# Sixteen experts on one core: row indices found two experts ahead, rows gathered one ahead, and a second norm in steps

## The chip, the cores and the metric

The kernel runs on one core of a Trainium2 chip. The metric is the device time of one execution in microseconds; the kernel before takes 2919.67 us (median of 3 runs, 2919.27 to 2936.29). The engines are TensorE (PE, matmuls, with PEld for its weight loads), VectorE (DVE), ScalarE (ACT), GpSimd (POOL) and SyncE (SP, which issues plain DMAs). Each works through its own list of instructions in order and waits for the others by semaphores.

## The reference

One layer of an encoder for 2048 tokens of 1024 channels, all float32. Four mixers (retention, RWKV-7, RG-LRU, gated linear attention) run side by side on the channels of a normed input; an output projection and a residual follow. Then comes the part that the change touches, in which each of 16 experts takes the 256 tokens with the largest affinity for it:

```python
def _expert_choice_ffn(x, router_w, router_b, w_gate, w_up, w_down):
    ...
    gates, idx = lax.top_k(jnp.swapaxes(aff, 1, 2), cap)
    bidx = jnp.arange(B)[:, None, None]
    xs = x[bidx, idx]
    hid = jax.nn.silu(jnp.einsum('becd,edf->becf', xs, w_gate)) * jnp.einsum('becd,edf->becf', xs, w_up)
    out = jnp.einsum('becf,efd->becd', hid, w_down) * gates[..., None].astype(x.dtype)
    return jnp.zeros_like(x).at[bidx, idx].add(out.astype(x.dtype))
```

Its result is added to the residual, and a final norm over the channels of each token gives the output.

## The kernel before

The mixers, the output projection and the choice of tokens (`top_k`) take the time up to about 1700 us. They are the same in both kernels. The rest is `experts` (L1441).

*Precision.* A float32 product is made as three products of float32r parts. `split` (L41) copies a tile to its high part on ACT (L43) and subtracts it on DVE for the low part (L44). `mm3` (L122) then issues three matmuls of 128 x 256 for each of eight row tiles (L129).

*Weights.* Each expert reads twelve tiles of 1 MB: four quarters each of gate, up and down. `weights` (L1448) loads one into x_st by SP and splits it into x_wh (ACT) and x_wl (DVE), each with three buffers.

*The choice of rows.* `select(e)` (L1458) does four things in one piece. DVE writes sixteen tiles x_oh that mark which token stands at which place of expert e (L1462, one buffer). PE multiplies them with the token numbers, 32 small products (L1466). DVE turns the sums into x_idx (L1468, L1469). Then POOL gathers the 256 rows of the normed tokens from g.hf into x_xs by two indirect DMAs (L1471, in `gather`, L1576). PE turns x_xs in 16 transposes (L1478), four to a bank of PSUM (two such banks), and ACT and DVE split each bank into x_xh and x_xl.

*The loop over experts (L1485).* For each expert: 384 gate and up products in eight groups of 48. After each group ACT makes the silu (x_sg), DVE multiplies, and the result is split into x_hh and x_hl. Then `select(e + 1)` is called (L1505), and then come 192 down products in four quarters, whose results ACT scales by the gate into x_os (L1527). The row scales stand in x_xs, so x_xs (two buffers) is in use until the expert's last x_os. Two scatter-adds (L1543, L1585) by POOL add x_os to g.acc in DRAM, the second after the first has landed.

*The final norm.* `final_norm` (L1564) norms 256 tokens at a time beside experts 11 to 13. Tokens that get more from experts 11 to 14 are normed again by `renorm` (L1588): gather from g.acc into fn_x (two buffers), squares on ACT (fn_sq, L1560), rstd and scaling on DVE, scatter to the output. L1509 does it for experts 11 to 13 in expert 14, and for 14 in expert 15:

```python
        while late and e >= NE - 2:
            renorm(g, late.pop())
```

The rows of expert 15 itself are normed as its down products finish (L1529 to L1541).

*What sets the order.* The program is not put on the engines as it is written. A scheduler goes through it with a simulated timeline and decides which instruction of each engine's list stands next. So a call that is written between gate and down products can end up among the down products, and the listing below shows the result.

Of the kernel before, what the change touches and what calls it, by code (L numbers as in the profile page):

```python
# [17 lines left out]
P = 128  # L18
# [6 lines left out]
IN_XA = 3328                # columns of w_in of the GLA decay's input  # L25
# [15 lines left out]
def split(g, hi, lo, src, pool=False):  # L41
    """hi + lo == src exactly, both exact in float32r."""
    g.nc.scalar.activation(out=hi, in_=src, func=AF.Copy)  # L43
    (g.nc.gpsimd if pool else g.nc.vector).tensor_tensor(out=lo, in0=src, in1=hi.bitcast(F32), op=OP.subtract)  # L44
# [6 lines left out]
def rstd_of(g, pool, ss, n, scale, eps, name):  # L51
    """1 / sqrt(ss * scale + eps) for [P, n] sums of squares: a guess from the bits of the
    number (within 4%), and three Newton steps, which leave 1e-10 of that."""
# [14 lines left out]
def head_norm(g, pool, y, n, center, eps):  # L68
    """Normalises y [P, n, 64] over the last axis, in place."""
# [14 lines left out]
def load_h_block(g, b):  # L84
    """Normalised, transposed, split activations of 512 tokens."""
# [36 lines left out]
def mm3(g, out, lhs, rhs, lsl, rsl, nk=KD):  # L122
    """out = lhs.T @ rhs over nk row tiles in three float32r passes; outs and lsls may be
    lists, the outs then parts of one bank (the first start clears it for all)."""
# [7 lines left out]
def proj_cm(g, w, n, h, store):  # L132
    """channel-major projections of a 512-token block"""
    for m0 in range(0, n, P):
        m = min(P, n - m0)
        ps = bank(g)
        mm3(g, ps[:m, :], w, h, slice(m0, m0 + m), slice(0, 512))
        o = g.op.tile([P, 512], F32, name="o_cm", tag="o_cm")
        g.evac(o[:m, :], ps[:m, :])
        store(m0 // P, o[:m, :])  # L140
        yield
# [12 lines left out]
def stage_proj(g, d):  # L154
# [6 lines left out]
    # channel-major: lru input and gate, gla q and k, the gates of retention and gla  # L161
# [37 lines left out]
    def pair(js, blocks, then=(None, None), loaded=False):  # L199
        """Two sets of columns; a block of activations is replaced while the other one is used."""  # L200
# [40 lines left out]
# ----------------------------------------------------------------- RWKV-7  # L241
C = 64
NB = T // P
RS = 256                  # tokens of one elementwise step
HALF = 10 * C             # of one block's row of the RWKV scratch: r1 k1 b1 b0 k0 r0, z, v with its chunks swapped, of two heads
# [4 lines left out]
def rwkv_consts(c):  # L250
# [4 lines left out]
    # strict masks are negative: the triangular systems are kept as I - N  # L255
    c["m_at"] = np.stack([-(p < j).astype(f), -(p > j).astype(f)], 1)            # [P, dir, 64]
# [48 lines left out]
def rwkv_a(g, dr, t0, ao):  # L305
    """Elementwise work of RS tokens in direction dr, the products of the triangular
    systems, all of it left in DRAM scratch block by block."""
# [20 lines left out]
    other = None                   # the other direction's bonus, when it has been here before  # L328
# [6 lines left out]
    def chunks(q, u):  # L335
        """chunks u and 5 - u of half q"""
# [29 lines left out]
    # sigmoid(u) = (1 + tanh(u / 2)) / 2: aa is kept as twice the sigmoid less one, k and en carry the factors 2 and 1/2  # L366
    nc.gpsimd.tensor_scalar(out=sw, in0=sw, scalar1=0.5, scalar2=0.5, op0=OP.mult, op1=OP.add)
    # decay inside each chunk
# [13 lines left out]
    # norm of kk  # L382
# [42 lines left out]
    # decay of every chunk, the channels of each head on both halves of the partitions  # L425
    nc.vector.tensor_copy(out=g.pcx[:, dr, t0 // P:t0 // P + nb, :, :, :].rearrange("p b q h n -> p h q b n"),
                          in_=ps[:, 0:4 * nch].rearrange("p (h q b n) -> p h q b n", h=2, q=2, n=2))
    # bonus
# [12 lines left out]
    # the triangular systems  # L441
# [27 lines left out]
def rwkv_inv(g, n, eng):  # L469
    """Inverts the triangular systems of 4 blocks of each direction.  On the partitions: direction, half of the  # L470
    system (that with no other to wait for first), chunk, block, head; as in ao the chunks are swapped."""
# [20 lines left out]
def rwkv_join(g, n, ao, pool, bl):  # L492
    """The remaining quarter of each inverse, from its diagonal blocks x0, x1 and the quarter ao of the
    system: x0 ao x1."""
# [4 lines left out]
    def blocks(c, dr, r, k):  # L499
        """rows r, columns k of the inverses of chunk 1 - c"""  # L500
# [36 lines left out]
def rwkv_b_buffers(g):  # L537
    """Buffers whose fixed parts are written once."""
# [46 lines left out]
def rwkv_prep(g, dr, b, loaded, res):  # L585
    """Everything of one 128-token block that does not wait for the state: the matrix
    that takes [state; values] to [outputs; next state] for each chunk and head.  Chunk 0
    keeps the state on partitions 0..63, chunk 1 on 64..127."""
# [4 lines left out]
    bk = [[ld[:, HALF * q + 192 - 128 * e:HALF * q + 320 - 128 * e] for e in range(2)] for q in range(2)]     # b and k of a chunk, b where the chunk is  # L593
# [27 lines left out]
    rd = turn(g.rd)                # r of two heads, block-diagonal: half, 1 - chunk, head  # L621
# [71 lines left out]
def weave(*gens):  # L693
    """Generators with the number of steps of each, in proportion."""
# [20 lines left out]
def rwkv_b(g):  # L715
# [4 lines left out]
    for i in range(1, NB + 2):  # L720
# [26 lines left out]
        # tokens that both directions have passed: norm now, the rest a round later  # L747
# [11 lines left out]
def rwkv_out(g, m):  # L759
    """Norm, bonus and gate of 256 tokens."""  # L760
# [28 lines left out]
# ----------------------------------------------------------------- retention  # L789
def ret_consts(c):  # L790
    i = np.arange(128)
    f = np.float32
    rel = (i[None, :] - i[:, None]).astype(f)          # [j, i]: i - j
# [16 lines left out]
PI_1 = 6.28125                          # 2 pi in three parts, the first two exact in products  # L810
# [6 lines left out]
def ret_tables(g):  # L817
# [3 lines left out]
    lgs = pool.tile([P, 2, 2], F32, name="rt_lgs")        # [direction, q]: heads 2 q and 2 q + 1 on the halves of the partitions  # L821
# [3 lines left out]
    # positions -> sine and cosine  # L825
# [6 lines left out]
    g.cs = pool.tile([P, NB, 2, 32], F32, name="rt_cs")    # cos, cos  # L832
    g.sn = pool.tile([P, NB, 2, 32], F32, name="rt_sn")    # -sin, sin
# [15 lines left out]
    # decays  # L849
# [21 lines left out]
def rotate(g, pool, b, src, n):  # L871
    """Rotary embedding of n heads of 64 in src."""
# [11 lines left out]
def retention(g):  # L884
    """Blocks of 128 tokens; a first sweep from the right for the backward states, a second
    one from the left for the rest.  Two heads share the partitions: their states and
    queries are block-diagonal."""
# [15 lines left out]
    def state(e, b, rk, v):  # L903
        """S becomes the state after block b"""
# [69 lines left out]
def gated_out(g, pool, y4, j, gate, gn, k0):  # L974
    """mixed rows k0, k0 + 1 of 512 tokens: y * gn * silu(gate), channel-major"""
# [12 lines left out]
# ----------------------------------------------------------------- RG-LRU  # L988
def lru(g, q):
# [18 lines left out]
    # s8 = -8 softplus(-lambda): max(-l, 0) + log1p(exp(-|l|)), the logarithm by its series in y / (2 + y)  # L1008
# [20 lines left out]
    # convolution over t - 2 .. t + 1  # L1029
# [9 lines left out]
    for dr in range(2):  # L1039
# [13 lines left out]
        # 1 - a^2 = tanh(-log a) (1 + a^2)  # L1053
# [16 lines left out]
# ----------------------------------------------------------------- GLA  # L1070
# [7 lines left out]
GB = 2                      # blocks of 128 tokens in one elementwise step  # L1078
# [3 lines left out]
def gla(g):  # L1082
# [13 lines left out]
    cc = big.tile([P, 2, 3, NB], F32, name="gl_cc")     # decays up to a block's middle, of a block, from its middle on  # L1096
    SX = big.tile([P, NB, HD], F32, name="gl_SX")
    S = [big.tile([P, HD], F32, name=f"gl_S{e}") for e in range(2)]      # [(head, k), v]
# [3 lines left out]
    def piece(j):  # L1102
        """decayed q and k of GP tokens in both directions, centred on the middle of each block"""
# [45 lines left out]
    def products(o, e, v):  # L1149
        """keys times values of the piece's blocks, which the states take up"""  # L1150
# [12 lines left out]
    def state(e, b, kv):  # L1163
        """S becomes the state after block b"""
# [3 lines left out]
    def diag(e, b, src):  # L1168
        """the state decayed to the middle of block b, block-diagonal"""
# [271 lines left out]
def experts(g):  # L1441
# [43 lines left out]
    for e in range(NE):  # L1485
# [23 lines left out]
        while late and e >= NE - 2:  # L1509
            renorm(g, late.pop())  # L1510
# [261 lines left out]
```

## Time and profile before

| | |
|---|---|
| time, median of 3 runs | 2919.67 us (2919.27 to 2936.29) |
| span of the profiled execution, first to last instruction | 2917.0 us |
| PE busy | 2575.3 us, 88% of the span |
| DVE, ACT, POOL busy | 1803.9, 1380.3, 731.2 us |
| DMA | 525.83 MB, 180 GB/s |

The page gives the profiled execution's span, and no other time of its own; the median of the timed runs is 2.7 us above that span. A matmul's end in the trace is modelled and matmuls overlap, so the busy time of PE is not read as speed; the starts of the matmuls and their number in a stretch are. The granted clock of PE has two levels, 1.00 (2.4 GHz) and 0.50 (1.2 GHz).

### The profile page before, as it was taken

The page shows a single profiled execution, that of the slowest core. Times are in us where ns is not written, and L with a number is a line of the kernel's source. Part 1 is how long each engine was busy: PE and PEld are TensorE (multiplying, and loading weights), DVE is VectorE, ACT ScalarE, POOL GpSimd, SP SyncE. Part 2 cuts the span into 40 slices and gives each one's busy share as a digit, 9 for nine tenths or more (in the row PEclk, how much of TensorE's full clock was granted, in tenths as well). Part 3 has the DMA queues.
Part 4 walks back from the last instruction along what each step waited for, and adds up shares of the span by engine and source line. Part 5 has one row for each costly group of instructions (what it writes and reads, how often), then busy time and mean ns, then how long its engine had stood idle before and what let it go on. Part 6 is the DMA issues. An engine that isn't in the chain of part 4 may idle for free. (4 is left out here: it accounts for less than half of the span.)

```text
span 2917.0 us, 47393 instructions
## 1 busy us (share of the span) xinstructions
PE 2575.3 (88%) x18433; PEld 2306.9 (79%) x18433; DVE 1803.9 (62%) x3462; ACT 1380.3 (47%) x2303; POOL 731.2 (25%) x764
## 2 busy tenths in 40 slices
PE   7999998888878898895899659999999999999987
PEld 5886686667667787774677459999999999999987
DVE  4244467878888778788654565555555555566655
ACT  4126666545534676555433224444444444454453
POOL 0001112544544554436534300000000000000121
PEclk9999999999988899897999879999999999999999
DMA  9342255576455554435254426666666666688874
GB/s 319 116 157 90 101 184 174 194 218 196 123 138 158 166 164 149 141 122 187 88 185 148 160 88 199 201 197 205 206 208 203 198 193 193 212 295 273 267 244 151
DMA packets 473569, 525.83 MB, mean 180 GB/s; under 512 B 129504, under 2 KB 415232, under 8 KB 472576
## 3 DMA queue, kind: packets, MB, share of 16 engines
q1 hardware_dynamic: 461536, 479.54, 50.7%
q0 software_dynamic: 11808, 43.26, 5.8%
q8 instruction: 145, 2.38, 0.3%
q14 instruction: 80, 0.66, 0.1%
HBM read 387.97 MB, written 136.84 MB: 180 GB/s over the span
## 5 line engine op out<-in xcount | busy, mean ns | idle before, releaser
L44 DVE TENSOR_TENSOR x_wl<-x_st,x_wh 128x2048 fp32r<-128x2048 f32 x189 | 432.9, 2291 | 342.6 <-ACT x_wh L43 342.2
L129 PE MATMUL bank<-x_xl,x_wh 128*128 128x256 f32 x2048 | 567.3, 279 | 0.0
L129 PE MATMUL bank<-x_xh,x_wh 128*128 128x256 f32 x2048 | 565.6, 279 | 1.9 <-ACT x_wh L43 1.8
L129 PE MATMUL bank<-x_xh,x_wl 128*128 128x256 f32 x2048 | 562.5, 279 | 2.0 <-DVE x_wl L44 1.8
L43 ACT ACTIVATE x_wh<-x_st 128x2048 fp32r<-128x2048 f32 x192 | 368.0, 1918 | 88.5 <-PE bank L129 69.1
L129 PEld LDWEIGHTS bank<-x_xh,x_wh 128*128 128x128 f32 x2048 | 387.2, 190 | 2.6 <-ACT x_wh L43 2.2
L129 PEld LDWEIGHTS bank<-x_xl,x_wh 128*128 128x128 f32 x2048 | 385.0, 188 | 0.0
L129 PEld LDWEIGHTS bank<-x_xh,x_wl 128*128 128x128 f32 x2048 | 381.4, 188 | 3.0 <-DVE x_wl L44 2.8
L129 PE MATMUL bank<-x_wh,x_hh 128*128 128x256 f32 x1024 | 290.4, 286 | 9.6 <-ACT x_hh L43 9.2
L129 PE MATMUL bank<-x_wl,x_hh 128*128 128x256 f32 x1024 | 293.8, 288 | 0.0
L129 PE MATMUL bank<-x_wh,x_hl 128*128 128x256 f32 x1024 | 291.3, 286 | 0.0
L129 PE MATMUL bank<-h_hi,w_hi 128*128 128x512 f32 x576 | 237.8, 415 | 24.7 <-DVE o_tm L1622 9.1
L129 PE MATMUL bank<-h_lo,w_hi 128*128 128x512 f32 x576 | 236.4, 410 | 0.0
L129 PE MATMUL bank<-h_hi,w_lo 128*128 128x512 f32 x576 | 233.9, 406 | 0.0
L1576 POOL DMA_INDIRECT x_xs<-hf,x_idx x32 | 51.5, 1608 | 617.6 <-issue 530.7
L129 PEld LDWEIGHTS bank<-x_wh,x_hh 128*128 128x128 f32 x1024 | 196.1, 192 | 10.0 <-ACT x_hh L43 9.4
L129 PEld LDWEIGHTS bank<-x_wl,x_hh 128*128 128x128 f32 x1024 | 197.8, 193 | 0.0
L129 PEld LDWEIGHTS bank<-x_wh,x_hl 128*128 128x128 f32 x1024 | 197.6, 193 | 0.0
L129 PE MATMUL bank<-w_hi,h_hi 128*128 128x256 f32 (+1 forms) x512 | 157.4, 307 | 28.2 <-DVE o_tm L1622 13.5
L129 PEld LDWEIGHTS bank<-h_hi,w_hi 128*128 128x128 f32 x576 | 111.4, 194 | 60.4 <-DVE o_tm L1622 10.6
L129 PE MATMUL bank<-w_hi,h_lo 128*128 128x256 f32 (+1 forms) x512 | 154.0, 301 | 0.0
L129 PE MATMUL bank<-w_lo,h_hi 128*128 128x256 f32 (+1 forms) x512 | 152.2, 297 | 0.0
(449 smaller groups left out, 5573.4 us busy)
## 6 DMA issues: line engine op xcount, KB each, us to landing
x_st<-in_exp_w_gate_dram SPq DMA_DIRECT2D x64, 1024.0 KB, 5.3
x_st<-in_exp_w_up_dram SPq DMA_DIRECT2D x64, 1024.0 KB, 5.5
x_st<-in_exp_w_down_dram SPq DMA_DIRECT2D x64, 1024.0 KB, 5.4
w_st<-in_w_in_dram SPq DMA_DIRECT2D x24, 1024.0 KB, 5.8
rw_sp<-sp SPq DMA_DIRECT2D x16, 1280.0 KB, 5.7
bld<-rw_sp SPq DMA_DIRECT2D x32, 640.0 KB, 5.1
ld<-rw_cm SPq DMA_DIRECT2D x14, 899.5 KB, 6.4
cm<-o_cm SPq DMA_DIRECT2D x40, 256.0 KB, 3.5
```

The costliest lines, as they stand in the source:

```text
L43: g.nc.scalar.activation(out=hi, in_=src, func=AF.Copy)
L44: (g.nc.gpsimd if pool else g.nc.vector).tensor_tensor(out=lo, in0=src, in1=hi.bitcast(F32), op=OP.subtract)
L129: g.nc.tensor.matmul(out, lhsT=lhs[a][:, k, lsl], rhs=rhs[b][:, k, rsl], start=(k + i == 0 and out is outs[0]), stop=(3 * k + i == 3 * nk ...
L1576: g.nc.gpsimd.indirect_dma_start(out=t[:, s], out_offset=None, in_=src, in_offset=bass.IndirectOffsetOnAxis(ap=idx[:, s:s + 1], axis=0))
```

## The change

`select` is cut into `places` (x_oh, products, x_idx), `fetch` (the gather) and `turned`, which turns a quarter of the rows at each step. The indices of expert e + 2 are found in expert e, between its gate and its down products. The rows of expert e + 1 are gathered when expert e begins, and turned in quarters after the second, third and fourth quarter of expert e's gate and up products and once more behind them. x_idx has six buffers where it had four.

`renorm` becomes `renorm_all`, a generator that gathers one expert's rows ahead of the norm of the one before. It makes one step after each quarter of the gate and up products and after each quarter of the down products of experts 14 and 15. Experts 11 to 13 are normed in that order, where it was 13 to 11. Comments and docstrings are dropped, which moves line numbers.

```diff
-    def select(e):
-        idx = g.exs.tile([P, 2], I32, name="x_idx", bufs=4)
+    def places(e):
+        idx = g.exs.tile([P, 2], I32, name="x_idx", bufs=6)
...
         nc.vector.tensor_tensor(out=idx, in0=pv, in1=ps[:, 1:4:2], op=OP.add)
+        return idx
+
+    def fetch(idx):
         xs = g.exs.tile([P, 2, HROW], F32, name="x_xs")
         gather(g, xs, g.hf, idx)
+        return xs
+
+    def turned(xs):
...
             split(g, hi[:, k:k + 2], lo[:, k:k + 2], ps.rearrange("p (m t) -> p m t", m=2))
-        return idx, xs, hi, lo
+            yield hi, lo
...
-    nxt = select(0)
+    idx = places(0)
+    xs = fetch(idx)
+    for xh, xl in turned(xs):
+        pass
+    ahead_idx = places(1)
     late, done, fss = [], [], {}
+    again = iter(())
     for e in range(NE):
-        idx, xs, xh, xl = nxt
+        if e + 1 < NE:
+            xs1 = fetch(ahead_idx)
+            turn1 = turned(xs1)
...
+            if e + 1 < NE and m:
+                xh1, xl1 = next(turn1)
...
+            if e >= NE - 2:
+                next(again, None)
         if e + 1 < NE:
-            nxt = select(e + 1)
+            xh1, xl1 = next(turn1)
+            nidx = places(e + 2) if e + 2 < NE else None
...
-        while late and e >= NE - 2:
-            renorm(g, late.pop())
...
+            if e >= NE - 2:
+                next(again, None)
         if e < NE - 1:
             scatter(g, g.acc, os, idx, compute_op=OP.add)
             if e >= NE - LATE:
                 late.append(idx)
+            if e == NE - 3 or e == NE - 2:
+                again = renorm_all(g, late)
+                late = []
+        if e + 1 < NE:
+            idx, xs, xh, xl = ahead_idx, xs1, xh1, xl1
+            ahead_idx = nidx
...
-def renorm(g, idx):
-    t = g.fn.tile([P, 2, D], F32, name="fn_x")
-    gather(g, t, g.acc, idx)
+def renorm_all(g, idxs):
+    ts = []
+    for idx in idxs:
+        t = g.fn.tile([P, 2, D], F32, name="fn_x")
+        gather(g, t, g.acc, idx)
+        ts.append((t, idx))
+        yield
+        if len(ts) == 2:
+            again(g, *ts.pop(0))
+            yield
+    while ts:
+        again(g, *ts.pop(0))
+        yield
+
+def again(g, t, idx):
     norm_rows(g, t, squares(g, t, 2))
     scatter(g, g.out, t, idx)
```

The scheduler makes the following of it. On PE, the first transposes of expert 1's rows (x_xs) stand in the kernel before among expert 0's down products (x_wh and x_wl with x_hh and x_hl), behind 79 of them and the 32 products with x_oh:

```order
L129 MATMUL bank<-x_wh,x_hl 128x256
L129 MATMUL bank<-x_wh,x_hh 128x256 x2
L1478 MATMUL bank<-c_ident,x_xs 128x128 x2
L129 MATMUL bank<-x_wl,x_hh 128x256
L129 MATMUL bank<-x_wh,x_hl 128x256
```

In the changed kernel they stand among the gate and up products (x_xh and x_xl with x_wh and x_wl):

```order
L129 MATMUL bank<-x_xl,x_wh 128x256
L129 MATMUL bank<-x_xh,x_wl 128x256
L1486 MATMUL bank<-c_ident,x_xs 128x128 x4
L129 MATMUL bank<-x_xh,x_wh 128x256
L129 MATMUL bank<-x_xl,x_wh 128x256
```

What moved: four transposes stand behind 192 gate and up products of the expert, four behind 288, and eight behind all 384. Then come 59 down products, the 32 products with x_oh for the expert after the next, and the other 133 down products. Before, the 32 products stood between gate and down products, and the transposes at four places among the down products.

On POOL, at the start of the expert stage, with the numbers of the tiles (x_idx_15202 and x_idx_15771 are those of experts 0 and 1, acc_82 is g.acc), before:

```order
L1576 DMA x_xs_15256<-hf_83,x_idx_15202 128x1040 x2
L1576 DMA x_xs_15825<-hf_83,x_idx_15771 128x1040 x2
L1585 DMA acc_82<-x_os_15858,x_idx_15202 2048x1024 x2
L1576 DMA x_xs_16625<-hf_83,x_idx_16571 128x1040 x2
L1585 DMA acc_82<-x_os_16658,x_idx_15771 2048x1024 x2
```

And in the changed kernel, where x_idx_15289 is expert 1's and x_idx_15858 expert 2's:

```order
L1603 DMA x_xs_15256<-hf_83,x_idx_15202 128x1040 x2
L1603 DMA x_xs_15343<-hf_83,x_idx_15289 128x1040 x2
L1612 DMA acc_82<-x_os_15912,x_idx_15202 2048x1024
L1603 DMA x_xs_16143<-hf_83,x_idx_15858 128x1040 x2
L1612 DMA acc_82<-x_os_15912,x_idx_15202 2048x1024
L1612 DMA acc_82<-x_os_16712,x_idx_15289 2048x1024
```

What moved: the gather of expert 2's rows stands between the two scatter-adds of expert 0, where it stood behind both, and needs indices that were found an expert earlier.

On ACT, in expert 15, whose second norm of expert 14's rows is fn_sq of fn_x (the squares of its two halves), before:

```order
L1498 ACTIVATE x_sg_27687<-bank_27638 128x256
L43 ACTIVATE x_hh_27570<-x_sg_27687 128x256
L1498 ACTIVATE x_sg_27753<-bank_27704 128x256
L43 ACTIVATE x_hh_27570<-x_sg_27753 128x256
L43 ACTIVATE x_wh_27820<-x_st_27818 128x2048
L1560 ACTIVATE fn_sq_28059,fn_ss_28058<-fn_x_28055 128x1024
L43 ACTIVATE x_wh_27934<-x_st_27932 128x2048
```

And in the changed kernel:

```order
L1513 ACTIVATE x_sg_27687<-bank_27638 128x256
L1587 ACTIVATE fn_sq_27816,fn_ss_27815<-fn_x_27692 128x1024
L43 ACTIVATE x_hh_27570<-x_sg_27687 128x256
L1513 ACTIVATE x_sg_27756<-bank_27707 128x256
L43 ACTIVATE x_hh_27570<-x_sg_27756 128x256
L43 ACTIVATE x_wh_27847<-x_st_27845 128x2048
L1587 ACTIVATE fn_sq_27818,fn_ss_27815<-fn_x_27692 128x1024
```

What moved: the first fn_sq stands directly behind the second x_sg of the expert, ahead of two x_hh and of the x_wh of the third up quarter; before, it stood behind them. On POOL the gather into that fn_x stands ahead of the gather into x_fx, where it stood behind it, and the third gather into fn_x in expert 14 stands behind two scatters to the output, where it stood behind three.

## Rows read from the trace of the kernel before

**Rows 1.** The page, busy tenths of PE in 40 slices of the span.

```profile
PE   7999998888878898895899659999999999999987
```

**Rows 2.** Waits of PE, 1750 to 2917 us: total us, times, longest us.

```profile
PE bank L1478 <- DMA x_xs<-hf,x_idx: 36.8, 13, 3.4
PE bank L129 <- ACT x_hh L43: 9.2, 1, 9.2
PE bank L129 <- DVE x_wl L44: 1.8, 3, 0.8
PE bank L129 <- ACT x_wh L43: 1.8, 2, 1.4
```

**Rows 3.** Timeline of PE, 2065.8 to 2071: start, us, line; in brackets idle before.

```profile
2066.55 0.39 PE L129 MATMUL bank<-x_wh,x_hh 128*128 128x256 f32 x2
2069.91 0.42 PE L1478 MATMUL bank<-c_ident,x_xs 128*128 128x128 f32 x2 [2.97 <-DMA x_xs<-hf,x_idx]
```

**Rows 4.** Timeline of POOL: gathers of two experts, scatter-adds between them.

```profile
2061.64 2.20 POOL L1576 DMA_INDIRECT x_xs<-hf,x_idx  x1 [38.88 <-issue]
...
2085.86 1.61 POOL L1585 DMA_INDIRECT acc<-x_os,x_idx  x1 [20.76 <-ACT x_os L1527]
2092.91 1.59 POOL L1585 DMA_INDIRECT acc<-x_os,x_idx  x1 [5.43 <-DVE x_hl L44]
2133.32 2.50 POOL L1576 DMA_INDIRECT x_xs<-hf,x_idx  x1 [38.83 <-issue]
```

**Rows 5.** Timeline of DVE, 2054 to 2072.

```profile
2058.05 2.44 DVE L1462 TENSOR_SCALAR x_oh<-x_iota,tk_slot 128x256 bf16<-128x256 bf16 x12
...
2060.66 2.29 DVE L44 TENSOR_TENSOR x_wl<-x_st,x_wh 128x2048 fp32r<-128x2048 f32 x1
```

**Rows 6.** Windows: length, busy us (instructions) of PE, PEld, DVE, ACT, POOL, PEclk, DMA, GB/s.

```profile
1924.68:1928.10 3.42, 3.42 (x19) 3.42 (x18) 1.17 (x1) 3.42 (x6) 0.00 (x0) 0.50 0.02 5
1928.10:1931.51 3.41, 3.41 (x31) 3.41 (x31) 3.40 (x4) 2.31 (x3) 0.00 (x0) 1.00 0.29 92
...
2658.55:2665.38 6.83, 5.64 (x27) 5.67 (x28) 1.42 (x1) 4.09 (x6) 0.00 (x0) 0.50 0.58 237
2808.74:2818.98 10.24, 4.64 (x21) 4.64 (x22) 4.58 (x15) 4.92 (x8) 3.67 (x4) 0.50 0.67 249
```

**Rows 7.** Windows, L129 on PE alone: busy us (matmuls), PEclk, DMA, GB/s.

```profile
1730.00:1750.00 20.00, 20.00 (x179) 1.00 0.64 210
...
2236.00:2256.00 20.00, 20.00 (x172) 1.00 0.73 207
```

**Rows 8.** Timeline of ACT in experts 14 and 15.

```profile
2811.12 1.06 ACT L1560 ACTIVATE fn_sq<-fn_x 128x1024 bf16<-128x1024 f32 x1 [12.01 <-DMA fn_x<-acc,x_idx]
...
2813.89 0.40 ACT L43 ACTIVATE x_hh<-x_sg 128x256 fp32r<-128x256 f32 x1
...
2851.51 0.39 ACT L1498 ACTIVATE x_sg<-bank 128x256 f32<-128x256 f32 x1 [1.82 <-PE bank L129]
...
2853.10 1.92 ACT L43 ACTIVATE x_wh<-x_st 128x2048 fp32r<-128x2048 f32 x1 [0.30 <-PE bank L129]
2858.28 1.06 ACT L1560 ACTIVATE fn_sq<-fn_x 128x1024 bf16<-128x1024 f32 x1 [3.26 <-DMA fn_x<-acc,x_idx]
```

**Rows 9.** DMA issues, 1750 to 2917 us: last column median us to landing.

```profile
x_xs<-hf,x_idx POOLq DMA_INDIRECT x30, 6.9
...
out_dram<-fn_x,x_idx POOLq DMA_INDIRECT x8, 6.5
```

**Rows 10.** Timeline of POOL in experts 14 and 15.

```profile
2791.20 0.98 POOL L1585 DMA_INDIRECT out_dram<-fn_x,x_idx  x1 [3.92 <-issue]
...
2802.77 0.98 POOL L1576 DMA_INDIRECT fn_x<-acc,x_idx  x1 [0.30 <-issue]
...
2848.26 1.52 POOL L1576 DMA_INDIRECT x_fx<-acc,x_idx  x1 [5.60 <-DMA acc<-x_os,x_idx]
...
2851.36 0.94 POOL L1576 DMA_INDIRECT fn_x<-acc,x_idx  x1 [0.30 <-issue]
```

## The prediction

> **What bounds the kernel now.** I read the page's busy slices first: from about 1750 us on, TensorE (PE) is busy in nine tenths or more of every slice [rows 1]. That stage is the sixteen experts, and what is won there must come out of PE's own time. So the next view is PE's waits in 1750 to 2917 [rows 2]. They are few and have names. Thirteen waits, 36.8 us together, are transposes of x_xs waiting for gathered rows. One wait of 9.2 us is a product waiting for x_hh. The waits for x_wl and x_wh make 3.6 us. All else is PE working.
>
> The timeline of PE at one of the thirteen shows the pattern [rows 3]: products run into 2066.55, the first transpose starts at 2069.91, and 2.97 us of idle time before it end with the landing of x_xs. Why so late? x_idx follows x_pv and a dozen x_oh on VectorE (DVE) [rows 5], GpSimd (POOL) issues the gather at 2061.64 [rows 4], and a gather lands a median 6.9 us after its issue [rows 9]. The list of places, the gather and the transposes of the next expert all lie between one expert's last gate product and its second down product, which is too little room.
>
> The granted clock shows a second cost of the same waits [rows 6]. In 1924.68 to 1928.10, right behind such a wait, it is 0.50 (the 1.2 GHz level) and 19 matmuls start or run; in the 3.41 us after that it is 1.00 (2.4 GHz) with 31. Seven such stretches of 3.41 us follow waits for x_xs, one of 6.83 us follows another (2658.55), and one of 10.24 us surrounds the wait for x_hh (2808.74).
>
> A third thing is in no list of waits. Windows that lie wholly among gate and up products, at full clock and with no idle time, hold 179 products of L129 in 20 us or 172 [rows 7]. Of eighteen such windows over all experts about half are of each kind. So 384 products cost 42.9 or 44.7 us, 1.8 us apart, by a level that changes after transposes, after the x_oh products and from one half of an expert to the next, and that I can't derive.
>
> **The change part by part.** *Places two ahead, gather one ahead.* Nothing is removed: 16 lists of 32 small products, 32 gathers and 256 transposes remain. The order shows the gather of expert e + 2 on POOL behind one scatter-add of expert e. In rows, a scatter-add's first half issues at 2085.86 and its second at 2092.91, because the second waits for the first to land [rows 4]; the two gathers (2.2 us for the first, less than that for the other) fit into that pause, so the scatter-adds lose nothing. The rows are then asked for about 3 us after an expert begins, land at about 3 + 2.5 + 6.9 = 12 us, and are first used behind 192 products, 192 x 0.117 = 22 us. That is 10 us to spare, so the thirteen waits go: -36.8.
>
> *Their half clock.* The clean stretch lost (31 - 19) / 31 x 3.41 = 1.3 us. Seven of them are 9.2. The longer ones had PE busy 5.64 and 4.64 us at the same rate, 2.2 and 1.8. Sum -13.2.
>
> The Trainium skill, "TensorE: Matmul & The Clock Gate", section "HAM oscillation — how this bites in real kernels", prices such time at half of the stretch's length. By that the 41 us of half clock cost 20.5 us, and the forecast would be 7 us lower, 2857. The matmul counts above disagree, since part of each stretch is the wait itself.
>
> *Places in the down products.* In the new order the x_oh products stand behind 59 down products, and x_pv waits for them on DVE. Queued behind x_pv are sixteen x_oh (2.44 us for 12, so 3.25), x_idx and the x_wl of the fourth down quarter (2.29) [rows 5]: 5.9 us with x_pv. PE needs that x_wl after 85 more products, 10 us. So 4 us are to spare, cost 0; if this cover went, each microsecond would be paid by 14 experts. The x_hh of the last eighth now stands behind two x_xh copies on ScalarE (ACT), but the order puts 58 down products that don't need it ahead of those that do, 6.8 us, for a chain of about 2.5 us. Cost 0.
>
> *Second norm, expert 14.* Now ACT sits at fn_sq until 2811.12 and x_hh follows only at 2813.89 [rows 8]; that is the 9.2 us. The third gather of this norm was issued at 2802.77, behind three scatters. In the new order it stands behind two, of which the second issued at 2791.20 [rows 10], and needs the buffer that these two empty, 6.5 us by the landing of out_dram<-fn_x [rows 9]. So it goes out near 2798 or earlier, 5 to 10 us sooner, and the wait shrinks to between 0 and 4. I take 1: -8.2. The other small waits (3.6) come from fn_sq in ACT's way; the order moves most fn_sq behind later products. Between -3.6 and +2 I take -1.9.
>
> *Second norm, expert 15.* Here the order speaks against the change. Before, fn_sq ran at 2858.28 behind the x_wh of 2853.10, and PE never waited. Now the first fn_sq stands directly behind the second x_sg, ahead of x_hh, x_sg, x_hh and that x_wh. Its gather takes the place of x_fx at 2848.26 [rows 10] and lands 6.9 us later by the pair 2851.36 to 2858.28, or 8.4 by the pair 2802.77 to 2811.12. Then ACT needs 1.1 + 0.4 + 0.4 + 0.5 + 0.4 to reach x_wh, at 2858 to 2859.5, done 1.9 later, x_wl another 2.3 later: 2862 to 2864. The order lets PE make 227 products before it needs that x_wl. The third x_sg, which started at 2851.51 when PE let it go [rows 8], stands behind 153 of them, so PE is there at 2851.5 + 74 x 0.117 = 2860. Cost 2 to 4, I take +3, and one stretch of half clock behind it, +1.3.
>
> Sum: -36.8 - 13.2 - 8.2 - 1.9 + 3 + 1.3 = -55.8. The level of the gate and up products I leave at half and half, 0, with bounds of 8 experts x 1.8 = 14 us to either side. The profiled execution has a span of 2917.0 us and the timed median is 2919.7, so 2.7 us lie around it: 2919.7 - 55.8 = 2864.
>
> **The rivals.** *All products on the dear level* (14%). The order now puts 192 gate and up products of each expert ahead of its first transpose, with x_oh products as the last thing before them, and expert 15, which had no transposes among or behind its gate products, ran at the dear level throughout (one of the 172). Against it: expert 0 had transposes among its gate products and ran at the cheap one (1730 to 1750) [rows 7]. Time 2864 + 14 = 2878. *All on the cheap level* (12%): transposes after products 192 and 288 would set it. Time 2850.
>
> *The rows come late all the same* (6%). If POOL's gathers stood behind both scatter-adds, or x_xs were still being read, they would go out at 10 us or later and land near 20 to 25, at the very place of the first transpose. Then the waits move from the down products into the gate products and the clock falls with them. What is left of the gain is the second norm's: 2914. The order on POOL speaks against it. This is also the case in which the change doesn't do what it says.
>
> *Slower* (3%): DVE's stop at x_pv. It holds four x_wl in a row. If x_oh took long enough, or x_wh came so late, that the fourth quarter's x_wl missed by 4 + 6 = 10 us, 14 experts would lose 6 us each, 84 - 56 = +28: 2948. It decides from a delay of 4 us on and makes the kernel slower than before from about 8. For it speaks only that DVE now stops where it did not; against it, that every row behind the 5.9 us above was taken beside a busy PE.
>
> **How the numbers follow.** My forecast holds with 62%, the rivals as given; 3% are left for a second norm whose waits grow beyond the bounds. The level's 14 us to either side and about 5 for the norm set the range, 2846 to 2886; it holds the forecast and both levels, and leaves the other cases out. 1% of the time, 29 us, is about what a measurement of this kernel can tell from no change. Faster by over 1% means below 2890: the forecast and both level cases, 0.88. Within 1%: the late rows and a part of the rest, 0.09. Slower: 0.03.
>
> **What would show it.** Right: PE's waits for x_xs of experts 1 to 14 gone, no granted clock of 0.50 between 1750 and 2650, the interval between the same gather of two experts 68 to 71 us where it was 71.7 from 2061.64 to 2133.32 [rows 4], a wait of 2 to 4 us for x_wh or x_wl in expert 15, and x_hh's wait under 4. Wrong: waits for x_xs between gate products; x_wl waits near the end of every expert's down products; 172 products per 20 us everywhere, or 179.

## The result and the profile after

The changed kernel takes 2892.35 us (median of 4 runs, 2892.16 to 2899.41), the kernel before 2921.89 (4 runs, 2919.27 to 2936.29): ratio 0.9898, with a 95% interval of 0.9871 to 0.9925. The forecast was 2864, with a range of 2846 to 2886. The change makes the kernel faster by 1%, some 29.5 us, about half of the 55.8 that were forecast, and the time lies above the range.

First the page of the changed kernel: busy tenths of PE in 40 slices of the span, and the granted clock.

```profile
PE   6999998888878898886899849999999999999997
PEclk9999999989997899987899969999999999999999
```

As in [rows 1], the experts are the stretch of nines at the end. The waits of PE in them, 1750 us to the end, in the columns of [rows 2]:

```profile
PE bank L129 <- ACT x_hh L43: 4.8, 1, 4.8
PE bank L129 <- ACT x_wh L43: 2.3, 2, 1.3
PE bank L129 <- DVE x_wl L44: 1.1, 2, 0.8
```

The 36.8 us of x_xs in [rows 2] are gone to the last microsecond. GpSimd's timeline shows why, beside [rows 4]:

```profile
2006.12 1.58 POOL L1612 DMA_INDIRECT acc<-x_os,x_idx  x1 [63.49 <-ACT x_os L1546]
2008.01 1.00 POOL L1603 DMA_INDIRECT x_xs<-hf,x_idx  x1 [0.30 <-ACT x_wh L43]
2009.32 1.86 POOL L1603 DMA_INDIRECT x_xs<-hf,x_idx  x1 [0.30 <-issue]
2012.66 1.71 POOL L1612 DMA_INDIRECT acc<-x_os,x_idx  x1 [1.48 <-DMA acc<-x_os,x_idx]
...
2081.05 1.86 POOL L1603 DMA_INDIRECT x_xs<-hf,x_idx  x1 [0.30 <-issue]
```

The two gathers lie between the halves of a scatter-add, 2.8 us behind the first gate product of this expert (2005.2), and the products of L129 run on to 2028.1 before the first transpose: the rows land about 8 us after the second gather, near 2018, so there are ten microseconds to spare, as forecast. But from one expert's second gather to the next one's are 2081.05 - 2009.32 = 71.73 us; in [rows 4], with the waits, they were 71.68. An expert without its wait takes as long as one with it.

Where the wait went, one row shows. These are the windows 1750 to 2650 (length, busy us and matmuls of PE, granted clock, DMA share, GB/s), first of the kernel before, then of the changed one:

```profile
1750.00:2650.00 900.00, 867.32 (x7670) 0.99 0.68 212
```

```profile
1750.00:2650.00 900.00, 900.00 (x7843) 1.00 0.69 218
```

PE is now busy without a gap and the clock is full, so 900 / 867.32 = 1.038 times the matmuls should stand there, and a little more for the clock. There are 1.023 times as many. Each product has become dearer, and the windows that answer to [rows 7] say by how much (L129 on PE, wholly among gate and up products):

```profile
2006.00:2026.00 20.00, 20.00 (x169) 1.00 1.03 298
2077.50:2097.50 20.00, 20.00 (x169) 1.00 1.02 294
```

Before, such a window held 179 products or 172. Now it holds 169, and so it does in every expert. The timeline of PE in one of them:

```profile
2009.85 0.28 PE L129 MATMUL bank<-x_xh,x_wh 128*128 128x256 f32 x1
2009.97 0.28 PE L129 MATMUL bank<-x_xl,x_wh 128*128 128x256 f32 x1
2010.09 0.28 PE L129 MATMUL bank<-x_xh,x_wl 128*128 128x256 f32 x1
2010.21 0.28 PE L129 MATMUL bank<-x_xh,x_wh 128*128 128x256 f32 x1
```

The starts are 0.12 us apart, with no wait, at full clock. Taken over all starts of the experts, the mean interval between products (those under 150 ns) went from 115.54 to 119.97 ns for gate and up, and from 117.46 to 119.91 for down products. That is a third level. In the kernel before, stretches of 40 products stand near 113 ns or near 118, and none at 120.

In the last two experts ScalarE's timeline answers to [rows 8]:

```profile
2779.59 1.06 ACT L1587 ACTIVATE fn_sq<-fn_x 128x1024 bf16<-128x1024 f32 x1 [4.58 <-DMA fn_x<-acc,x_idx]
...
2783.55 1.06 ACT L1587 ACTIVATE fn_sq<-fn_x 128x1024 bf16<-128x1024 f32 x1 [2.81 <-DMA fn_x<-acc,x_idx]
...
2784.61 0.40 ACT L43 ACTIVATE x_hh<-x_sg 128x256 fp32r<-128x256 f32 x1
...
2825.35 1.06 ACT L1587 ACTIVATE fn_sq<-fn_x 128x1024 bf16<-128x1024 f32 x1 [8.67 <-DMA fn_x<-acc,x_idx]
```

The squares of the third renormed expert still stand ahead of an x_hh that PE needs: this is the 4.8 us. Those of expert 15 stand where the order had them, ScalarE waits 8.67 us for their rows, and PE pays 1.8 us for it.

### The profile page after: what moved, and what is told of

Same layout as the page of the kernel before. It is cut to its first block, busy times and chain, and to the rows that moved or that the text cites. A ratio compares the mean times of both kernels' runs of the same rounds, so it can differ in the third digit from the quotient of the medians.

```text
span 2890.1 us, 47361 instructions
## 1 busy us (share of the span) xinstructions
PE 2596.1 (90%) x18433; PEld 2332.7 (81%) x18433; DVE 1802.5 (62%) x3462; ACT 1382.8 (48%) x2303; POOL 719.4 (25%) x764
## 4 chain that ended last, share of the span: by engine, by line
PE 46%; DVE 4%; DMA 2%; issue 1%; ACT 1%; POOL 1%; SPq 0%; POOLq 0%; ACTq 0%; DVEq 0%
PE bank L129 42%; PE bank L1486 1%; DMA fn_x<-acc,x_idx 1%; DVE tk_j L1389 1%; PE bank L1467 1%; PE bank L1323 0%; DVE tk_c L1398 0%; PE bank L1328 0%; DVE hn_t L63 0%; ACT x_wh L43 0%; DVE hn_t L62 0%; DMA wo_x<-in_x_dram 0%; DVE rt_a L878 0%; DMA rt_ld<-tm 0%; DVE x_wl L44 0%
## 5 line engine op out<-in xcount | busy, mean ns | idle before, releaser
L129 PE MATMUL bank<-x_xh,x_wh 128*128 128x256 f32 x2048 | 580.6, 285 | 2.4 <-ACT x_wh L43 2.3
L129 PE MATMUL bank<-x_xl,x_wh 128*128 128x256 f32 x2048 | 578.1, 283 | 0.0
L129 PE MATMUL bank<-x_xh,x_wl 128*128 128x256 f32 x2048 | 572.7, 283 | 1.1 <-DVE x_wl L44 1.1
L129 PEld LDWEIGHTS bank<-x_xh,x_wh 128*128 128x128 f32 x2048 | 393.8, 192 | 3.2 <-ACT x_wh L43 2.7
L129 PEld LDWEIGHTS bank<-x_xl,x_wh 128*128 128x128 f32 x2048 | 393.7, 192 | 0.0
L129 PEld LDWEIGHTS bank<-x_xh,x_wl 128*128 128x128 f32 x2048 | 390.3, 192 | 1.5 <-DVE x_wl L44 1.5
L129 PE MATMUL bank<-x_wh,x_hh 128*128 128x256 f32 x1024 | 290.2, 285 | 4.8 <-ACT x_hh L43 4.8
L129 PE MATMUL bank<-x_wl,x_hh 128*128 128x256 f32 x1024 | 291.4, 285 | 0.0
L129 PE MATMUL bank<-x_wh,x_hl 128*128 128x256 f32 x1024 | 289.9, 284 | 0.0
L1612 POOL DMA_INDIRECT acc<-x_os,x_idx x30 | 48.5, 1617 | 927.1 <-ACT x_os L1546 898.8
L129 PE MATMUL bank<-h_hi,w_hi 128*128 128x512 f32 x576 | 237.2, 414 | 21.2 <-DVE o_cm L1662 8.8
L129 PE MATMUL bank<-h_lo,w_hi 128*128 128x512 f32 x576 | 235.8, 409 | 0.0
L129 PE MATMUL bank<-h_hi,w_lo 128*128 128x512 f32 x576 | 233.4, 405 | 0.0
L129 PEld LDWEIGHTS bank<-x_wh,x_hh 128*128 128x128 f32 x1024 | 196.6, 193 | 5.0 <-ACT x_hh L43 5.0
L129 PEld LDWEIGHTS bank<-x_wl,x_hh 128*128 128x128 f32 x1024 | 197.5, 193 | 0.0
L129 PEld LDWEIGHTS bank<-x_wh,x_hl 128*128 128x128 f32 x1024 | 197.4, 193 | 0.0
L129 PE MATMUL bank<-w_hi,h_hi 128*128 128x256 f32 (+1 forms) x512 | 161.1, 315 | 23.5 <-ACT o_tm L1664 11.0
L129 PE MATMUL bank<-w_hi,h_lo 128*128 128x256 f32 (+1 forms) x512 | 156.8, 306 | 0.0
L129 PEld LDWEIGHTS bank<-h_hi,w_hi 128*128 128x128 f32 x576 | 111.1, 193 | 56.1 <-DVE o_cm L1662 10.2
L129 PE MATMUL bank<-w_lo,h_hi 128*128 128x256 f32 (+1 forms) x512 | 155.3, 303 | 0.0
```

Of the source, the lines that this page charges most:

```text
L129: g.nc.tensor.matmul(out, lhsT=lhs[a][:, k, lsl], rhs=rhs[b][:, k, rsl], start=(k + i == 0 and out is outs[0]), stop=(3 * k + i == 3 * nk ...
L1612: g.nc.gpsimd.indirect_dma_start(out=dst, out_offset=bass.IndirectOffsetOnAxis(ap=idx[:, s:s + 1], axis=0), in_=t[:, s], in_offset=None, **kw)
```

## The experiments

**The theory.** The diff has one edit that no step of the prediction spoke of. x_idx gets 6 buffers in place of 4, and what lies behind it in the partition moves. The built programs list where each tile starts (bytes within a partition, first buffer; the other buffers lie multiples of 8,192 further on):

```
            x_wh     x_wl     x_xh     x_xl     x_hh     x_hl
before      64384    88960   138560   154944   189760   197952
changed     64384    88960   138624   155008   189824   198016
```

Two buffers of 32 bytes move x_xh, x_xl, x_hh and x_hl by 64. Each product has a stationary operand, which PEld loads, and a moving one, which streams through; in `mm3` they are lhsT and rhs, and a row of the trace names the moving one first. For gate and up products x_wh or x_wl is stationary and x_xh or x_xl moves; for down products x_hh or x_hl is stationary and x_wh or x_wl moves. Counted within 128 bytes, the tiles of x and h stood 64 behind the w-tiles and now stand 0 behind them. Below, "distance" is this number. Theory A: the distance sets the level of the products. Theory B: the order of TensorE's work does, the transposes between gate products, as the rivals of the prediction had it.

**Only the move, on the kernel before.**

```diff
-        idx = g.exs.tile([P, 2], I32, name="x_idx", bufs=4)
+        idx = g.exs.tile([P, 2], I32, name="x_idx", bufs=6)
```

> The kernel before with nothing changed but the number of x_idx buffers, 4 to 6, which no instruction waits for; it moves every tile behind them in the partition up by 64 bytes, x_xh, x_xl, x_hh and x_hl among them, and leaves x_wh and x_wl where they are. Theory A (the level of the products is set by where the stationary and the moving operand lie to each other): the gate and up products start 120 ns apart as in the changed kernel, 166 or 167 per 20 us, and the time rises by about 9,216 x (120.0 - 116.8) = 29 us, to 2940 to 2955 us. Theory B (the level is set by the order of TensorE's work, the transposes between gate products): nothing changes, 2915 to 2925 us, windows of 172 and of 179 products.

Measured: 2945.81 us (9 runs) against 2924.05 for the kernel before beside it; ratio 1.0061, interval 1.0035 to 1.0086. The windows read as in the changed kernel:

```profile
2024.00:2044.00 20.00, 20.00 (x169) 1.00 0.95 256
```

The level is 119.99 ns for gate and up products and 119.86 for down products, with no instruction of the change there. Theory B falls. In the traces PE's experts, from the first gate product to PE's end, take 29.2 us longer (1184.7 to 1213.9). The level alone makes 34 of that, and the waits gave some back:

```profile
PE bank L1478 <- DMA x_xs<-hf,x_idx: 32.8, 13, 3.1
PE bank L129 <- ACT x_hh L43: 7.5, 1, 7.5
```

In [rows 2] they were 36.8 and 9.2. Slower products leave the gather more time. Why the medians differ by 22 us and not by 29 isn't shown; single runs of the kernel before spread over 25 us (2916.55 to 2941.43).

**The move taken back, on the changed kernel.**

```diff
-        idx = g.exs.tile([P, 2], I32, name="x_idx", bufs=6)
+        idx = g.exs.tile([P, 2], I32, name="x_idx", bufs=8)
```

> The changed kernel with 8 buffers of x_idx in place of 6: the same tiles move up by another 64 bytes, 128 in all against the kernel before. Theory A: the level goes back to that of the kernel before, 113 or 118 ns, and the time falls by 18 to 60 us below 2892, near 2863. Theory B: 2892 us, 120 ns.

Measured: 2858.47 us (2852.96 to 2860.35), ratio 0.9772 to the kernel before, interval 0.9727 to 0.9816. The same instructions in the same order as in the changed kernel, 34 us faster. The window of 1750 to 2650, and two among gate and up products (20 and 10 us):

```profile
1750.00:2650.00 900.00, 900.00 (x8141) 1.00 0.72 230
```

```profile
1995.00:2015.00 20.00, 20.00 (x179) 1.00 1.03 299
2016.70:2026.70 10.00, 10.00 (x86) 1.00 0.64 214
```

8,141 matmuls are 1.061 times those of the kernel before. Both of the old levels are back: 179 in 20 us, and behind the transposes 86 in 10.

**Only the down products' operands moved**, by a tile of 64 bytes at the head of the pool of x_hh and x_hl:

```diff
     again = iter(())
+    nc.gpsimd.memset(g.exh.tile([P, 16], F32, name="x_pad"), 0.0)
```

> The changed kernel with a tile of 64 bytes ahead of x_hh and x_hl alone (written once, 0.1 us on GpSimd). Theory A: gate and up products stay at 120 ns, the 3,072 down products fall to 118 or 113 ns, 7 to 20 us less: 2872 to 2886 us. Theory B: 2892 us.

Measured: 2881.17 us (2871.74 to 2884.87). Gate and up products stay at 119.98 ns, down products fall to 113.77. This is theory A in one kernel, with its other half as control.

**All moved together**, by the same tile at the head of the weights' pool, so that x_xh starts at the address which it has with 8 buffers:

> The changed kernel with a tile of 64 bytes ahead of all tiles of the weights: x_wh, x_wl, x_xh, x_xl, x_hh and x_hl all move up by 64 bytes together, so x_xh starts at the very address that it had with 8 buffers of x_idx, but its distance to x_wh is that of the changed kernel. Theory A1 (the distance of the two operands sets the level): 120 ns and 2885 to 2900 us. Theory A2 (the place of x_xh and x_hh by itself sets it): 113 to 118 ns and 2850 to 2870 us, as with 8 buffers.

Measured: 2898.2 us (2894.04 to 2900.33), 119.95 and 119.93 ns. With 8 buffers x_xh stood at the same address and the level was another; and in the changed kernel with 8 buffers x_wh stands where it does with 6. So neither address sets the level by itself; the distance does (theory A1).

**The control for the buffers themselves**: the kernel before with 8 of them.

> The kernel before with 8 buffers of x_idx in place of 4: the operands move by 128 bytes, so their distance within 128 is what it was. Theory A1: 113 and 118 ns in turns as before, 2910 to 2930 us. Rival (the buffers of x_idx themselves, or any move of the tiles, cost): 2940 us or more, as with 6.

Measured: 2916.25 us (10 runs) against 2923.5, ratio 0.9971, interval 0.9945 to 0.9997. No stretch stands at 120 ns. The cheaper of the two old levels even prevailed (mean 114.0 and 113.9 ns), yet little came of it:

```profile
PE bank L1478 <- DMA x_xs<-hf,x_idx: 42.8, 15, 4.0
PE bank L129 <- ACT x_hh L43: 5.9, 1, 5.9
PE bank L129 <- ACT x_wh L43: 5.1, 3, 2.2
```

The intervals of its products say 9,216 x some 2.2 ns = 20 us less. The waits for x_xs and x_wh took back 42.8 - 36.8 + 5.1 - 1.8 = 9.3 of them, the wait for x_hh gave 9.2 - 5.9 = 3.3, and the half clock behind the waits took more; in the trace PE's experts are 8.2 us shorter.

**Other distances.** With 7 and 9 buffers of x_idx the distance is 32 and 96; for 48 there are 7 buffers as well, and the four tiles are made 32 elements longer and used from their fifth element on (in the kernel with the held norm, below, which takes 2842.65 us).

> The changed kernel with 7 buffers of x_idx: the tiles move up by 32 bytes, half the step between the two placements known. Theory A says only that the level may differ from 120 ns; if lines of 64 bytes matter, a start in the middle of one costs as much or more (2892 us or above), if only the distance of the two operands matters it lies between (2860 to 2892 us). Theory B: 2892 us.

> The changed kernel with 9 buffers of x_idx: x_xh stands 96 bytes behind x_wh, counted within 128. If the level depends on the distance alone and to either side alike, 96 is like 32: 116.7 ns for gate and up products, 118.3 for down products, 2870 to 2882 us. If it matters which of the two is ahead, it is another level between 113 and 120 ns: 2850 to 2892 us.

> The kernel with the held second norm and x_xh, x_xl, x_hh and x_hl 48 bytes behind x_wh and x_wl (counted within 128) in place of 64. Distances of 0, 32, 64 and 96 gave 120, 117, 113 or 118, and 120 ns. If the level falls evenly from 32 to 64, it is near 115 ns throughout and the time 2843 to 2850 us; if it is the least in between, at or under 113 ns, 2815 to 2835 us; if only whole steps of 32 bytes are told apart, 117 ns and 2855 to 2865 us.

Measured: 2874.91 us (2872.14 to 2882.79) with 7 buffers, 2895.98 (2891.98 to 2899.83) with 9, 2878.24 (2873.73 to 2882.41) at 48. The time with 7 buffers lies in the span given for the distance. That with 9 lies above both of its spans and that at 48 above all three, so what I expected of symmetry, and of how the level runs from 32 to 64, was wrong. The mean intervals between starts, in ns:

| distance | kernel | gate, up | down |
|---|---|---|---|
| 0 | changed; before with 6 buffers; all moved | 119.97; 119.99; 119.95 | 119.91; 119.86; 119.93 |
| 32 | changed with 7 buffers | 116.7 | 118.3 |
| 48 | held norm, shifted | 118.8 | 119.7 |
| 64 | before; before with 8; changed with 8 | 115.5; 114.0; 115.8 | 117.5; 113.9; 114.3 |
| 96 | changed with 9 buffers | 120.0 | 118.9 |

Only at 64 is any stretch at 113 ns, and there it alternates with 118. That the distance counts within 128 bytes, and not within 256, rests on the kernels at 64: within 256 the kernel before stands at 192 and those with 8 buffers at 64, and both show the same two levels. The kernels at 0 all stand at 0 within 256 as well.

**One of two moving operands moved**: a tile of 64 bytes between x_xh and x_xl. I took x_xl for a stationary operand when I wrote what I expected; in these products it is the moving one, and the stationary x_wh and x_wl stay where they are.

> The changed kernel with a tile of 64 bytes between x_xh and x_xl: x_xh stays at distance 0 from x_wh and x_wl (counted within 128), x_xl and behind it x_hh and x_hl go to 64. Of three gate or up products one has x_xl as its stationary operand. Theory P (a product is slow by the distance of the stationary operand that is loaded beside it, that of the next product): the step from the product of x_xh and x_wh to that of x_xl and x_wh falls to 113 ns, the other two stay at 120. Theory Q (by its own two operands): the step behind the product of x_xl falls, the others stay. Theory R (one level for all): all three between 113 and 120 alike. In each case down products at 113 ns as with the pad ahead of x_hh, so some 19 us for these and 0 to 14 us for the others: 2856 to 2882 us.

Measured: 2877.86 us (2871.69 to 2882.19), so within the span given, but the steps behind the three kinds of product are 118.8, 119.0 and 117.8 ns. With the roles put right, P and Q both say that the step behind the product of x_xl falls and the others stay. It is not so (119.0), so neither shows. The result is nearest to R, one level for all, and that level moves between 117 and 120 along an expert. Which pair of reads meets is left open by this.

**The second norm alone.** The kernel with 8 buffers, with `renorm` of the kernel before in place of `renorm_all`:

> The changed kernel with 8 buffers of x_idx and the second norm as it was before: three gathers and norms behind the gate products of expert 14, one of expert 15. It tells what the new norm is worth beside the kernel with 8 buffers (2858 us). Theory C (as predicted: the new norm takes 8 us off the wait for x_hh, 2 off smaller waits, and gives 4 back in expert 15): 2862 to 2868 us. Theory D (what the wait in expert 14 lost comes back as waits for x_wh in experts 14 and 15): within 3 us of 2858.

Measured: 2857.22 us (2855.97 to 2858.62), ratio 0.9774, interval 0.9742 to 0.9806, against 0.9772 with the new norm: theory D. The old norm's waits beside the new expert part,

```profile
PE bank L129 <- ACT x_hh L43: 7.1, 2, 6.6
PE bank L129 <- ACT x_wh L43: 4.7, 2, 2.8
PE bank L129 <- DVE x_wl L44: 0.4, 1, 0.4
```

and the new one's there,

```profile
PE bank L129 <- ACT x_hh L43: 5.5, 1, 5.5
PE bank L129 <- ACT x_wh L43: 4.5, 2, 3.1
PE bank L129 <- DVE x_wl L44: 1.2, 2, 0.8
```

come to 12.2 and 11.2 us. So what the change gained is the expert part's.

**The second norm held back.** The squares get as bias a zero that is worked out from a later tile, so that the order can't put them ahead of it:

```diff
+    z = g.fn.tile([P, 1], F32, name="fn_z")
+    g.nc.vector.tensor_scalar(out=z, in0=g.held, scalar1=0.0, scalar2=None, op0=OP.mult)
-    norm_rows(g, t, squares(g, t, 2))
+    norm_rows(g, t, squares(g, t, 2, z))
```

`g.held` is a column of the x_sg or x_os made last. The gathers of the first two experts are issued together, the first norm comes a quarter later, the third gather and the second norm another quarter later, the third norm in the second down quarter.

> The changed kernel with 8 buffers of x_idx, and squares of the second norm that can't start before a named later tile is there (x_sg of the second or third eighth pair, x_os of the second down quarter), by a zero worked out from that tile which they add as bias; so the squares can't stand on ScalarE ahead of products that TensorE needs. Theory E (the waits of 5.5 us for x_hh, 4.5 for x_wh and 1.2 for x_wl in the last two experts are all ScalarE's place in line for rows that have not landed): these waits fall below 2 us together, the half clock behind them goes, 2844 to 2850 us. Rival F (VectorE then waits in their place for the sums and x_wl comes late): 2855 to 2862 us.

Measured: 2842.65 us (2834.66 to 2847.88), ratio 0.9724, interval 0.9685 to 0.9763. PE's waits in its experts:

```profile
PE bank L129 <- ACT x_wh L43: 1.5, 1, 1.5
PE bank L129 <- DVE x_wl L44: 0.8, 1, 0.8
```

That is 2.3 us instead of 11.2, with no stretch of half clock among the experts: theory E, but for 0.3 us in the waits, and 1 us below the span of time. The run holds the squares and issues the gathers at other places, and it doesn't tell which of the two did how much. The kernel is 50 us faster than the changed one, 34 by the distance and 16 by this.

**Transposes 8 and 8.** The same with `next(turn1)` twice behind the second quarter and twice behind the fourth:

> The kernel with 8 buffers of x_idx and the held second norm, its sixteen transposes put behind the second quarter's gate and up products (8) and behind the fourth's (8), in place of 4, 4 and 8. At 64 bytes of distance the traces show that the products behind 4 transposes run at 118 ns and those behind 8 at 113. Theory G (the number of transposes between sets the phase of all that follows): all gate and up products but the first of the run at 113 ns, 15 x 192 x 4.5 ns = 13 us less than 2843: 2826 to 2834 us. Rival H (a stretch flips at every group whatever its size): the third and fourth quarter stay at 118 ns, or others go there, 2838 to 2855 us.

Measured: 2842.59 us (2833.67 to 2853.46): theory G falls. At the distance of 64, with these groups and with 4, 4 and 8, the products run at 118 ns from the first group of transposes of an expert to its last, then at 113 through the down products and half of the next expert, whether a group has 4 or 8 transposes. What picks the level at a distance of 64 is still open.

## Why the prediction was wrong

The intervals from one start on PE to the next, from the first gate product on (9,943 in either trace), split the loss by size:

| | before | after |
|---|---|---|
| over 300 ns: waits, mostly | 32, 59.7 us | 8, 10.7 us |
| 150 to 300 ns: half clock (139 and 22 of them), steps beside transposes | 237, 49.9 us | 101, 20.8 us |
| from the first gate product to PE's end | 1184.7 us | 1159.6 us |

The waits and the half clock lost 49.0 + 29.1 = 78.1 us, of which 160 intervals x 0.12 = 19 came back as plain products: -59. The level gave back 6,113 x 4.43 ns = 27.1 for gate and up and 2,876 x 2.45 = 7.0 for down products: +34. Together that is -25, the difference in the table's last row; PE also began the experts 1.8 us earlier, and the span is 26.9 shorter.

Point by point:

- *Places two ahead, gather one ahead: -36.8.* Right, mechanism and size. The rows landed a median 7.9 us after their issue, and no transpose of experts 1 to 15 waited.
- *Their half clock: -13.2.* Right in size. The stretches of 0.50 between 1750 and 2650 are gone; one of 6.83 us is left, around the wait for x_hh:

```profile
2783.31:2790.14 6.83, 5.08 (x24) 5.08 (x25) 4.86 (x16) 4.09 (x6) 1.09 (x2) 0.50 0.42 163
```

  The intervals of 150 to 300 ns became 136 fewer, 117 of them in these stretches: 29.1 - 136 x 0.12 = 12.8 us, for 41 - 6.8 = 34.2 us less of half clock.

  The Trainium skill, "TensorE: Matmul & The Clock Gate", section "HAM oscillation — how this bites in real kernels", prices such time at half of its length; an estimate by that is 17.1 us. The intervals of this trace give less, as the matmul counts did before.

  The prediction's reason for the difference, that part of each stretch is the wait itself, is only part of it: in six of the seven stretches of 3.41 us PE is busy throughout. The steps themselves don't double. In the kernel before, then in the changed one, at a granted clock of 0.50:

```profile
1926.53 0.41 PE L129 MATMUL bank<-x_wh,x_hh 128*128 128x256 f32 x1
1926.75 0.41 PE L129 MATMUL bank<-x_wl,x_hh 128*128 128x256 f32 x1
1926.96 0.41 PE L129 MATMUL bank<-x_wh,x_hl 128*128 128x256 f32 x1
...
2785.44 0.41 PE L129 MATMUL bank<-x_wl,x_hh 128*128 128x256 f32 x1
2785.65 0.41 PE L129 MATMUL bank<-x_wh,x_hh 128*128 128x256 f32 x1
2785.86 0.41 PE L129 MATMUL bank<-x_wl,x_hh 128*128 128x256 f32 x1
```

  The median step there is 213 ns in both kernels, against 113 to 120 at 1.00, so PE's busy time at half clock loses some 0.45 of its length. PE was idle for 5.6 of the 34.2 us; 28.6 x 0.45 = 12.9.
- *Places in the down products: 0.* Right. No wait for x_wl in experts 0 to 13, so the rival by x_pv did not come.
- *Second norm, expert 14: -8.2.* The direction was right, the size not: 9.2 became 4.8 where I took 1. The third gather was to go out 5 to 10 us sooner. It went out 50.9 us behind the first gate product of its expert (2722.6), where it had been 53.5 (2802.77 and 2749.3), so 2.6 sooner; it waited for the landing of the second scatter, which took some 8 us where I took 6.5:

```profile
2765.36 1.39 POOL L1612 DMA_INDIRECT out_dram<-fn_x,x_idx  x1 [3.15 <-issue]
2773.48 0.97 POOL L1603 DMA_INDIRECT fn_x<-acc,x_idx  x1 [6.73 <-DMA out_dram<-fn_x,x_idx]
```

  Beside the new expert part the old norm waits no longer than the new one (the run with the old norm), so the two terms of the second norm with the small waits and the half clock behind, -5.8 together, are nothing that can be measured.
- *Second norm, expert 15: +3 and +1.3.* Right place, but smaller than forecast: PE waited 1.8 us, and the clock stayed full, so the 1.3 did not come.
- *The level: "I leave at half and half, 0, with bounds of 8 experts x 1.8 = 14 us to either side".* This is the step that failed. It measured +34. The bounds were taken between the two levels that the kernel before shows, so the term could not be larger than the dear one everywhere, 2878; the rival "all products on the dear level" had the direction, but a cause, the transposes, that the runs refute. Both were ways of the order of work; the level changed by a line of the diff that I had read as bookkeeping, two more buffers of 32 bytes.

With 8 buffers in that line the time is in the range: 2858.47, 5.5 us below 2864. That it comes so close is in part luck. By the intervals of that trace the waits and the half clock gave 57 us, where the whole forecast was 55.8, though the second norm's part of it did not come; and the level was not that of the kernel before either, but 7 us cheaper, as more of the down products ran at 113 ns (mean 114.3, from 117.5). The interval between two gathers (forecast 68 to 71 us, measured 71.7) was the sign that would show it wrong, and so were the windows; "172 products everywhere, or 179" did not think of 169.

## What to carry to other kernels

A change of buffers is a change of addresses: before the order of the work is blamed, list where the operands start in both built programs, and see which distances have moved. Read a stage at full clock and without gaps by the number of products in a window; PE busy 900 of 900 us was 7,843 matmuls in one kernel and 8,141 in another. And a gain in a stage whose waits are set by a transfer's fixed path is partly eaten by these waits (the kernel before with 8 buffers), so waits go first, then the products' own time counts in full.

## What was not expected of the hardware

The step from one product to the next (128x128 stationary, 128x256 moving), at a granted clock of 1.00 and without waits, is 120.0 ns when the two operands start at the same place within 128 bytes. At 64 bytes between them it is 113.3 or 117.8 ns, in stretches. At 32 its mean is 116.7 (gate and up) and 118.3 (down), at 48 118.8 and 119.7, at 96 120.0 and 118.9. At 2.4 GHz the levels at 0 and 64 are 288 cycles, and 272 or 283. At a granted clock of 0.50 (1.2 GHz) the step is 213 ns, 256 cycles, both at 64 (the kernel before) and at 0 (the changed one): there the distance cost nothing.

One move of 64 bytes was worth 34 us of 2892, more than the change it came with brought on the whole. That the load of the next stationary operand and the stream of the moving one disturb each other in the memory would fit, as PEld runs beside PE in the windows of [rows 6]; this is argued and not shown, and the run that moved one of two moving operands did not tell which pair meets.
